# A reordered schedule line: the last two head groups of the first attention layer, row block 0 ahead of row block 1

## The chip, the cores and the metric

One NeuronCore of a Trainium2 chip runs the whole program. The metric is the device time in microseconds of one execution; several executions give a median. One more execution was recorded with the hardware profiler, and the trace rows below come from that one.

## The reference, cut to what matters

A decoder trunk of two layers works on 256 tokens of 1024 features, in float32. Layer 0 has causal attention with 16 heads of 64 (with 256 tokens there is one block, so the block-sparse attention is plain causal attention); layer 1 has differential attention. An MLP with 4096 hidden features follows each. Every sub-layer is modulated and closed in the same way:

```
mod = silu(c) @ ada_w + ada_b                       # six vectors of 1024 for each layer
for i in range(2):
    shift1, scale1, gate1, shift2, scale2, gate2 = split(mod[i], 6)
    h = x * (1 + scale1) + shift1
    y = attention(h) @ w_out                        # q, k, v = h @ w_in, rotary on 16 of 64 features
    x = layer_norm(alpha * x + (1 + gate1) * y)     # the closing of the attention
    h = x * (1 + scale2) + shift2
    y = square(relu(h @ w_up)) @ w_down
    x = layer_norm(alpha * x + (1 + gate2) * y)
```

## The kernel before, in words

The 256 tokens are two row blocks of 128, called b = 0 and b = 1. Each float32 product is made of three matmuls in a rounded format: every operand is split into a rounded part hi (ScalarE, L130 for weights) and a remainder lo (VectorE, L131), and hi·hi, hi·lo, lo·hi are accumulated. Weights come in by DMAs on SyncE's queue into three `raw` buffers; the split parts lie in eight `hi` and eight `lo` buffers of 128x1024.

`PROGRAM` is the order of the work, written out by hand, one string for each layer. A token is a step and its indices. `S0` to `S7` and `P`, `F` with the same numbers go through the pairs (b, g) in the order (0,0), (1,0), (0,1), (1,1), (0,2), (1,2), (0,3), (1,3), where g is a group of four heads; so even numbers are row block 0 and odd ones block 1.

- `Qbg`: the q and k columns of a group, 24 matmuls of 512 columns, then the rotary part on VectorE. `Tbg`: four transposes of the result.
- `Sn`: scores of the four heads (L417) into two banks with the tag `sc`, mask and maximum on VectorE (L381), exponential on ScalarE (L384).
- `Pn`: probabilities transposed (L397), copied by ScalarE (L399), multiplied with the values (L457), scaled on VectorE (L468). `Fn`: two transposes (L476), split into hi and lo (L482, L483).
- `Obh`: block b's part of the output product from head groups 2h and 2h+1, 24 matmuls (L184). `O00` and `O01` add up in two banks tagged `ac`, `O10` and `O11` in two tagged `sc`.
- `fN`: N steps of the filler. The filler is a list of the adaLN vectors: each step loads a 128x1024 piece of `ada_w` (L215, two buffers `aw`) and multiplies and sums it on VectorE (L216). For layer 0's attention the list holds GATE1, SCALE2, SHIFT2, eight pieces each. `B0` asks for what it needs of them (`need`), spreads the gate over the partitions (L115, L117), makes the columns A and B (L245 to L247) and loads `ln_g` and `ln_b`.
- `Cb0`: the closing of block b: gate and residual (L289, L292), statistics (L302, L303), the inverse root on GpSimd (L277, L278), normalisation (L308, L311), then eight transposes (L320), A and B applied by ScalarE (L324), and the split (L327, L328) into the tiles `hT` that the MLP multiplies.
- `Ubj`, `Xbj`, `Dbj`: the MLP's up product, its transposes and its down product for block b and columns j; `U` starts with L167.

The order of the string is not the order on an engine. It gives each instruction its rank; when the program is built, a planner walks through modelled time and gives each engine, among the instructions that it takes for ready, the one of the highest rank. From then on each engine works through its own list strictly in order. A buffer of a tag is handed out when its former user is done.

Of the kernel before, what the change touches and what calls it, by code (L numbers as in the profile page):

```python
# [44 lines left out]
PROGRAM = (  # L45
    """
    L0 V00 V10 Q00 T00 Q10 T10 Q01 T01 Q11 T11 S0 V01 f2 S1 f1 P0 S2 V11 f5 P1 F0 S3 P2 Q02 T02 f4 S4
    Q12 T12 f2 F1 f2 P3 S5 F2 Q03 T03 f4 P4 F3 S6 Q13 T13 f4 P5 F4 O00 P6 S7 F5 B0 P7 F6 F7 O01 C00 O10
    O11 C10 U00 U01 X00 U10 U11 X01 f1 X10 D00 f1 X11 Y2 f4 D10 f1 D01 f1 D11 Y3 f3 D02 f1 D12 Y4 f3 D03 f1
    D13 Y5 f3 D04 f1 D14 Y6 f3 D05 f1 D15 Y7 f2 D06 D07 B1 C01 D16 D17 C11  # L50
    """,
# [735 lines left out]
```

## Time and profile before

| what | value |
|---|---|
| three timed runs, us | 642.17, 645.62, 645.78 |
| median, us | 645.62 |
| the profiled execution, us | 644.11 |
| its span from first to last instruction, us | 640.7 |
| busy in the span: TensorE matmul, VectorE, ScalarE | 95%, 78%, 59% |

The span is what the trace shows; 3.4 us of the profiled execution's time lie outside it. PE is TensorE's matmuls, PEld its weight loads, which overlap them; DVE is VectorE, ACT ScalarE, POOL GpSimd and SPq SyncE's DMA queue. The matmuls are pipelined, so a row's duration (0.39 us for 512 columns) is longer than the distance to the next start.

### The profile page before, as it was taken

How to read it: one execution, taken by the hardware profiler on the slowest of the kernel's cores; microseconds unless marked ns; L12 is line 12 of the kernel's file. 1: busy time of each engine (PE TensorE's matmuls, PEld its weight loads, DVE VectorE, ACT ScalarE, POOL GpSimd, SP SyncE). 2: the span in 40 equal slices, each digit the busy share in tenths (PEclk: the TensorE clock that was granted, in tenths of full speed). 3: DMA queues.
4: the chain of work that ended last, by engine and by line, in shares of the span. 5: the costliest groups of instructions: out<-in, count | busy, mean ns of one | idle time of the engine just before them, and what ended most of it. 6: DMA issues, size and time to landing. Idle time of an engine off the chain costs nothing.

```text
span 640.7 us, 8768 instructions
## 1 busy us (share of the span) xinstructions
PE 609.0 (95%) x3140; PEld 499.6 (78%) x3140; DVE 500.4 (78%) x903; ACT 377.6 (59%) x699; POOL 22.2 (3%) x37
## 2 busy tenths in 40 slices
PE   4889999998999999999999999989999999999994
PEld 3667887886888888888877787767788888888883
DVE  5798998889978878888799989977984646465446
ACT  3448665657846545664477676765775556475530
POOL 0000000001000000000000010021100000000002
PEclk9999999999999999999999999999999999999998
DMA  8997998876689888989765967682663764746401
GB/s 292 406 322 279 313 325 286 288 250 227 215 309 343 308 313 330 326 294 338 268 231 188 337 229 263 232 289 68 208 218 109 259 225 143 255 133 213 182 0 66
DMA packets 65941, 158.23 MB, mean 247 GB/s; under 512 B 4041, under 2 KB 21098, under 8 KB 65898
## 3 DMA queue, kind: packets, MB, share of 16 engines
q1 hardware_dynamic: 65898, 157.68, 70.1%
q8 instruction: 24, 0.39, 0.2%
q14 instruction: 19, 0.16, 0.1%
HBM read 156.62 MB, written 1.05 MB: 246 GB/s over the span
## 4 chain that ended last, share of the span: by engine, by line
PE 64%; DVE 18%; DMA 6%; ACT 4%; issue 3%; POOL 2%; SPq 1%; DVEq 0%; POOLq 0%; ACTq 0%
PE ac L184 13%; PE sc L184 10%; PE mm L687 7%; PE tp L687 6%; DMA aw<-in_ada_w_dram 6%; DVE lo L131 5%; DVE aw L216 4%; PE mm L167 4%; PE mm L169 4%; PE mm L168 4%; PE mm L692 3%; PE tp L692 3%; ACT hi L130 2%; DVE z L292 1%; DVE z L289 1%
## 5 line engine op out<-in xcount | busy, mean ns | idle before, releaser
L131 DVE TENSOR_TENSOR lo<-raw,hi 128x1024 fp32r<-128x1024 f32 x196 | 232.0, 1197 | 44.1 <-ACT hi L130 40.4
L130 ACT CAST hi<-raw 128x1024 fp32r<-128x1024 f32 x196 | 201.3, 1034 | 62.5 <-PE sc L184 43.6
L216 DVE CUSTOM_DVE_ANT_0 aw<-aw,sbc,tabT 128x1024 f32<-128x1024 f32 x96 | 122.0, 1280 | 23.1 <-DMA aw<-in_ada_w_dram 22.7
L167 PE MATMUL mm<-hi,hT 128*128 128x512 f32 x224 | 90.6, 405 | 6.1 <-ACT hi L130 3.2
L169 PE MATMUL mm<-hi,hT 128*128 128x512 f32 x224 | 89.0, 398 | 0.0
L168 PE MATMUL mm<-lo,hT 128*128 128x512 f32 x224 | 88.6, 396 | 0.2 <-DVE lo L131 0.2
L687 PE MATMUL mm<-hT,hi 128*128 128x512 f32 x192 | 60.4, 396 | 0.0
L687 PE MATMUL tp<-hT,hi 128*128 128x512 f32 x192 | 60.3, 395 | 0.0
L167 PEld LDWEIGHTS mm<-hi,hT 128*128 128x128 f32 x224 | 42.3, 189 | 16.1 <-ACT hi L130 3.8
L184 PE MATMUL ac<-hi,sTh 128*128 128x512 f32 x160 | 51.2, 397 | 0.0
L184 PE MATMUL ac<-lo,sTh 128*128 128x512 f32 x160 | 50.8, 394 | 0.0
L184 PE MATMUL ac<-hi,sTl 128*128 128x512 f32 x160 | 50.4, 392 | 0.0
L169 PEld LDWEIGHTS mm<-hi,hT 128*128 128x128 f32 x224 | 42.3, 189 | 9.1 <-DVE hT L328 0.4
L168 PEld LDWEIGHTS mm<-lo,hT 128*128 128x128 f32 x224 | 42.3, 189 | 8.6 <-DVE lo L131 0.3
L184 PE MATMUL sc<-hi,sTh 128*128 128x512 f32 x144 | 45.3, 392 | 0.0
L184 PE MATMUL sc<-lo,sTh 128*128 128x512 f32 x144 | 45.1, 391 | 0.0
L184 PE MATMUL sc<-hi,sTl 128*128 128x512 f32 x144 | 44.6, 390 | 0.0
L692 PEld LDWEIGHTS tp<-hT,lo 128*128 128x128 f32 x192 | 34.4, 188 | 7.5
L692 PEld LDWEIGHTS mm<-hT,lo 128*128 128x128 f32 x192 | 34.4, 188 | 7.3
L697 ACT COPY nat<-mm 128x256 f32<-128x256 f32 x24 | 7.8, 376 | 52.4 <-PE mm L687 52.4
L692 PE MATMUL tp<-hT,lo 128*128 128x256 f32 x192 | 36.0, 279 | 0.0
L692 PE MATMUL mm<-hT,lo 128*128 128x256 f32 x192 | 35.9, 279 | 0.0
(153 smaller groups left out, 899.4 us busy)
## 6 DMA issues: line engine op xcount, KB each, us to landing
aw<-in_ada_w_dram SPq DMA_DIRECT2D x96, 512.0 KB, 5.5
raw<-in_mlp_w_up_dram SPq DMA_DIRECT2D x32, 1024.0 KB, 5.9
raw<-in_mlp_w_down_dram SPq DMA_DIRECT2D x32, 1024.0 KB, 5.1
raw<-in_diff_w_in_dram SPq DMA_DIRECT2D x16, 512.0 KB, 5.1
raw<-in_moba_w_in_dram SPq DMA_DIRECT2D x24, 256.0 KB, 5.5
raw<-in_moba_w_in_dram SPq DMA_DIRECT2D x8, 512.0 KB, 4.8
raw<-in_moba_w_out_dram SPq DMA_DIRECT2D x4, 1024.0 KB, 8.4
raw<-in_diff_w_in_dram SPq DMA_DIRECT2D x4, 1024.0 KB, 5.7
```

The costliest lines, as they stand in the source:

```text
L130: act.copy(out=hi[:, :n], in_=raw_ap)
L131: vec.tensor_tensor(out=lo[:, :n], in0=raw_ap, in1=hi[:, :n], op=ALU.subtract)
L167: pe.matmul(dst, lhsT=xh, rhs=wh, start=start, stop=False)
L168: pe.matmul(dst, lhsT=xh, rhs=wl, start=False, stop=False)
L169: pe.matmul(dst, lhsT=xl, rhs=wh, start=False, stop=stop)
L184: pe.matmul(dsts[h], lhsT=a, rhs=w[:, h * 512:(h + 1) * 512], start=start and k == 0 and i == 0, stop=stop and k == n - 1 and i == 2)
L216: vec.tensor_tensor_reduce(out=aw, in0=aw, in1=sbc, scale=1.0, scalar=adab_cols(l, v)[:, j:j + 1], op0=ALU.mult, op1=ALU.add, accum_out=dst)
L289: vec.tensor_tensor(out=z[:, c_], in0=accs[c_.start // 512][:, a0:a0 + c_.stop - c_.start], in1=gate[:, c_], op=ALU.mult)
L292: vec.scalar_tensor_tensor(out=z[:, c_], in0=xt[b][:, c_], scalar=ALPHA, in1=z[:, c_], op0=ALU.mult, op1=ALU.add)
L687: pe.matmul(ps, lhsT=w[k][0][:, c_], rhs=x3[k], start=first, stop=last)
L692: pe.matmul(ps[:, 0:S], lhsT=w[k][1][:, c_], rhs=x3[k][:, 0:S], start=False, stop=False)
L697: act.copy(out=r[:, i * S:(i + 1) * S], in_=ps[:, S:2 * S])
```

## The change

Only the third and fourth line of layer 0's string differ. The steps are the same and none is added or dropped; `F3`, `P5`, `F5`, `S7` and `Q13`, `T13` (block 1) go behind steps of block 0, and `C00`, which stood after all P and F, now stands ahead of `S7`.

```
     L0 V00 V10 Q00 T00 Q10 T10 Q01 T01 Q11 T11 S0 V01 f2 S1 f1 P0 S2 V11 f5 P1 F0 S3 P2 Q02 T02 f4 S4
-    Q12 T12 f2 F1 f2 P3 S5 F2 Q03 T03 f4 P4 F3 S6 Q13 T13 f4 P5 F4 O00 P6 S7 F5 B0 P7 F6 F7 O01 C00 O10
+    Q12 T12 f2 F1 f2 P3 S5 F2 Q03 T03 f4 P4 S6 F4 f4 O00 P6 Q13 F6 B0 O01 T13 F3 P5 C00 S7 F5 O10 P7 F7
     O11 C10 U00 U01 X00 U10 U11 X01 f1 X10 D00 f1 X11 Y2 f4 D10 f1 D01 f1 D11 Y3 f3 D02 f1 D12 Y4 f3 D03 f1
```

## Rows read from the trace of the kernel before

**Rows 1.** The page: busy time, share of the span, instructions.
```profile
PE 609.0 (95%) x3140; PEld 499.6 (78%) x3140; DVE 500.4 (78%) x903; ACT 377.6 (59%) x699; POOL 22.2 (3%) x37
```
**Rows 2.** Waits of PE, 50 to 640 us: us in total, times, longest.
```profile
PE tp L320 <- DVE nm L310: 1.8, 3, 1.0
PE tp L320 <- DVE z L308: 1.5, 3, 0.5
...
PE ac L457 <- ACT pT L399: 1.0, 1, 1.0
...
PE mm L168 <- DVE lo L131: 0.2, 1, 0.2
```
**Rows 3.** Timeline of PE at the closing: start, us, engine, line, operation.
```profile
143.24 0.62 PE L184 MATMUL sc<-hi,sTl 128*128 128x512 f32 x2
143.70 0.61 PE L184 MATMUL sc<-hi,sTh 128*128 128x512 f32 x2
145.27 0.63 PE L320 MATMUL tp<-cs,z 128*128 128x128 f32 x4 [0.96 <-DVE nm L310]
...
146.57 0.70 PE L184 MATMUL sc<-hi,sTl 128*128 128x512 f32 x2
148.40 0.50 PE L167 MATMUL mm<-hi,hT 128*128 128x512 f32 x1 [1.13 <-ACT hT L327]
```
**Rows 4.** Timeline of DVE at the closing.
```profile
123.00 0.42 DVE L381 CUSTOM_DVE_ANT_0 sc<-sc,cs 128x256 f32<-128x256 f32 x1
...
134.83 0.69 DVE L289 TENSOR_TENSOR z<-ac,gate 128x512 f32<-128x512 f32 x1 [0.52 <-PE ac L184]
...
141.32 1.28 DVE L216 CUSTOM_DVE_ANT_0 aw<-aw,sbc,tabT 128x1024 f32<-128x1024 f32 x1
...
143.73 0.16 DVE L247 TENSOR_TENSOR B<-B,col 128x8 f32<-128x8 f32 x1
144.58 0.55 DVE L308 TENSOR_SCALAR z<-z,bna,rs 128x512 f32<-128x512 f32 x1 [0.69 <-POOL rs L278]
```
**Rows 5.** Timeline of ACT: the last exponential of S7, and the closing.
```profile
126.18 0.46 ACT L384 ACTIVATE p<-sc,mx 128x256 f32<-128x256 f32 x1
...
146.01 1.83 ACT L324 ACTIVATE full<-tp,B,A 128x128 f32<-128x128 f32 x5
147.72 0.62 ACT L327 CAST hT<-full 128x512 fp32r<-128x512 f32 x1
```
**Rows 6.** Stages: PE, PEld, DVE, ACT, POOL busy; granted clock, DMA share, GB/s.
```profile
97.00:149.00 52.00, 48.13 (x299) 39.16 (x296) 43.90 (x100) 30.38 (x69) 1.65 (x2) 1.00 0.80 275
...
135.00:140.00 5.00, 5.00 (x24) 4.14 (x23) 4.54 (x8) 3.35 (x4) 0.00 (x0) 1.00 0.90 335
```
**Rows 7.** Timeline of PE: O00's first matmul and its ninth, Q13, S7, P7, F6.
```profile
101.01 0.47 PE L184 MATMUL ac<-hi,sTh 128*128 128x512 f32 x1
...
106.29 0.40 PE L184 MATMUL ac<-lo,sTh 128*128 128x512 f32 x1
...
108.06 0.48 PE L167 MATMUL mm<-hi,hT 128*128 128x512 f32 x1
...
113.97 0.39 PE L169 MATMUL mm<-hi,hT 128*128 128x512 f32 x1
...
121.53 1.16 PE L417 MATMUL sc<-qkT 64*128 64x128 f32 x16
...
129.40 1.89 PE L457 MATMUL mm<-v,pT 128*128 128x64 f32 x16
131.13 0.39 PE L476 MATMUL tp<-cs,on 128*128 128x128 f32 x2
```
**Rows 8.** The tile aw, 95 to 145 us: its operations, its landing.
```profile
L216 DVE CUSTOM_DVE_ANT_0 aw<-aw,sbc,tabT x13: 1274/1279/1286, 97.4 to 141.3; 128x1024 f32<-128x1024 f32 x13
...
DMA to landing us min/median/max: 4.0/4.9/5.5
```
**Rows 9.** Timeline of PE: the longest wait at the same place in layer 1.
```profile
432.91 0.44 PE L397 MATMUL tp<-cs,p 128*128 128x128 f32 x2 [0.85 <-DVE sTl L486]
```

## The prediction

> **What bounds the kernel now.** I read the page first [rows 1]: PE has matmuls in flight for 95% of the span, no other engine comes near. A high share alone does not say that PE is the limit, so the second view is the list of PE's waits after the first products [rows 2]: 14 rows from 1.8 down to 0.2 us, 10.5 us together. The reader is to see two things there: from 50 us on PE waits for almost nothing, so a reordering can give back some 10 us in all and not more; and the largest rows name the closing (z and nm). The third view is PE's timeline at layer 0's closing [rows 3]. Two matmuls of 512 columns take 0.46 us there (143.24 to 143.70), 0.23 each. O01's sums are done when the closing's first product starts, 134.83 [rows 4]; the first matmul of U00 starts at 148.40. Between them lie the dense matmuls of O10 and O11, and twice PE stands: 143.70 to 145.27 is 1.57 us for two matmuls worth 0.46, so 1.11 lost; 146.57 to 148.40 is 1.83 for 0.46, so 1.37 lost. The closing of block 0 (from O01's end to U00, 13.5 us) is a little longer than the work that covers it. This is what the change aims at, and it is 2.5 us.
>
> The fourth view, the stages [rows 6], is the warning: from 97 to 149 us DVE is busy 43.9 of 52 us, 84%. A closing is itself mostly DVE work. It does not move into a stretch where its engine rests.
>
> The Trainium skill (Perfetto Trace Analysis, Identifying the Most-Contended Engine) says that matmul busy time is a poor measure of how near TensorE is to its limit and that the busy share of the weight loads is a good one. By it the stretch has 25% of room, since PEld is busy 39.16 of 52 us; the fourth rival below prices that reading from rows.
>
> **The change part by part.** No instruction is added or removed, so every engine's sum stays; only positions move, and with them waits. The DMAs keep their order on SP's queue: the filler pieces of both f4, then the rows of w_out for O00, then the last two pieces and the two broadcast loads of B0, then the rows for O01, stand in that sequence in both strings. GpSimd has only the two short operations of each closing.
>
> (a) C00 ahead of S7, F5, P7, F7. What now covers it: O10 and O11 as before, 13.5 minus 2.5 us lost is 11.0 us of PE work, and in addition the pieces of block 1 that come after O01. S7 is 1.2 us, P7's 16 value matmuls are 1.73 us (129.40 to 131.13) [rows 7] and its 8 transposes about 0.9 by 0.11 each, so 2.6; P5 is the same shape, 2.6; two F some 0.2 each. That is 6.8 us, so the cover is 17.8 us. The chain is 13.5 us; if S7's mask and maximum on DVE (four operations of 0.42 us and a little more [rows 4]) all go in between, it is 15.4. Both are under 17.8: the two stalls go, minus 2.5 us.
>
> (b) What is late next: the column B. The shift needs the last of the 24 filler pieces. In the trace that product starts at 141.32 and B is made at 143.73 [rows 4], 0.85 us before the normalisation itself. ACT then needs four applications (0.37 each, 1.83 for five) and a cast of 0.62 [rows 5], 2.1 us, so U00 could start at 143.9 + 2.1 = 146.0. PE without its two stalls would be there at 148.4 - 2.5 = 145.9. So the saving of (a) just fits, if this stream stays where it is. It has two buffers: a landing of 4.9 us and a product of 1.28 give one piece each 3.1 us, while the 12 distances from 97.4 to 141.3 are 3.66 each [rows 8]. It could end 6.8 us earlier at best; if DVE takes the pieces later, it ends later. Were the transposes placed before B is there, ACT would stand at its first L324, and in its list behind that wait are the pT copies for P7 and the hi parts of the MLP's first weights, for which PE and DVE wait in turn. The second f4 has moved ahead of O00 and Q13 in rank, which speaks for a little earlier. I take no change, ends -0 and +2.5 (the whole of (a)).
>
> (c) Q13 behind O00 and P6. O00 was the filler that PE used from 101 to 127 us. At 108.06, when Q13 starts, 9 of its 24 matmuls are done (101.01 to 106.29) [rows 7] and 15 are left, 3.4 us; with P6's 1.3 us they now go first, so Q13 moves back by up to 4.7 us, from its end at 114.2 to 118.9, and T13 and S7 with it: S7 from 121.53 to at most 126.2. Its softmax ends 5.1 us after its scores start (121.53 to 126.64) [rows 5, 7], at most 131.3. Until then O10 cannot start, because its banks are those of the scores. What PE has between 118.9 and then: O01 5.5, P5 2.6, the gate's 8 transposes 0.9, T13 0.5, S7 1.2, F3 and F5 0.4, together 11.1 us, to 130.0. So between 0 and 1.3 us of new wait, and more where DVE lets the closing go ahead of S7's softmax: C00 has the higher rank now, and its two gate products, two additions, two statistics and one aggregate are at least 4.1 us (six of 0.69 by the first). Ends 0 and +5.4. The nearest row for a tail of this kind is the longest wait at the same place in layer 1, 0.85 us [rows 9], where the closing and the last P lie equally near each other. The planner sees the DVE conflict too and can put the softmax first when z is not ready. I take +0.5, near the lower end, for that reason.
>
> (d) The split of w_out's second half. Its hi buffers come free as Q13 uses up the group's weights, so these splits move back with Q13, and O01 with them; that is inside the 11.1 us of (c) and hides behind P5 and P6. At nothing if so; if not, it is the same starvation as in (c). More or fewer switches between kinds of matmul cost about 0.1 us each (0.48 us for the first matmul of Q13, 0.39 for its last [rows 7]); ten more or fewer is 1 us either way, taken as 0.
>
> (e) C10 keeps its cover: U00 and U01, 11.0 us behind O11, as before. The MLP and layer 1 keep their order. 0.
>
> Sum: -2.5 + 0 + 0.5 + 0 + 0 = -2.0 us. The profiled execution took 644.11 us with a span of 640.7, so the sum gives a span of 638.7 and 642.1 us. That execution lies 1.5 us under the median of the runs shown, 645.62; against the median the forecast is 643.6.
>
> The Trainium skill (Perfetto Trace Analysis, Optimization Strategy) says that interleaving regimes with different most-contended engines can improve performance. Here the row speaks half against it: after PE, DVE is the busiest engine on both sides of the interleaving [rows 6], so by the rule the gain would be the full 2.5 us, by the row 2.5 less what DVE gives back.
>
> **The rivals.** First, **the shift stream holds the closing** (b): z is ready early, but B is not, or the planner's ready times give nearly the old order on the engines. Then PE waits at U00 as it does now and the time is 645.6, within 1 us. For it: B lies 0.85 us ahead of the normalisation today. Against it: the arithmetic of (b) leaves room for 2.4 us.
>
> Second, on the other side, **PE starves between O01 and O10**: S7's softmax stands behind C00 on DVE, the banks stay taken, and O00, which used to fill such holes, is spent. Price: 1.3 + 4.1 us of new wait. It decides from the point where S7's last exponential ends later than 130.0 us, when PE has used up O01 and P5. With the 2.5 saved it is +2.9, 648.5; if the stream of (b) also slips and nothing is saved, +5.4, 651.0. For it: DVE at 84% and the lost filler. Against it: the planner ranks only what is ready, so the softmax goes first wherever z is not.
>
> Third, **all waits of the region go**: besides the 2.5 us also the wait of 0.96 for pT and the smaller ones [rows 2], and a microsecond of switches. That is up to -5, 640.6.
>
> Fourth, **PE is far from full**: the weight loads fill only 75% of the stretch, so a better mixture could pack it tighter by 12.8 us, 632.8. Against it: in 135 to 140 us PE waits for nothing, starts a matmul each 0.23 us or less, and PEld is busy 4.14 of 5 us [rows 6], so 83% is full here and the room is 52 - 39.16 / 0.83 = 4.8 us. This is the reading of the page named above, and by it the trace disagrees as far as 100% is taken for full.
>
> **How the numbers follow.** The forecast (-1 to -4) has 0.50, the stream rival 0.22, starvation 0.20, all waits gone 0.06, the fourth 0.02. The likeliest gives 643.6. Runs of the same kernel spread by 3.6 us (642.17 to 645.78). The lower end of the range is 640.6 less a microsecond of that spread, 639.5; the upper takes in the first price of starvation, 648.5, and a microsecond, 649.5. Outside are about 1 in 10 above and 1 in 10 below. Faster by over 1% means below 639.2, slower means over 652.1; 1% is about what a measurement of this kernel can tell from no change. Faster: the fourth rival and the edge of the third, 0.06. Slower: both of starvation's parts together and more, 0.07. Within: 0.87.
>
> **What would show it.** Right: in PE's timeline no wait for nm at the first L320 and none for hT at the first L167 of the MLP, which starts at about 146 us; L289 on `ac` before S7's L381 or among them; P7 and F7 later than the start of C00. B's L247 still at 141 to 144. Wrong by (b): L320 early, then L324 on ACT waiting for B. Wrong by (c): a wait of PE of over 1 us between 118 and 132, ended by an exponential, a pT copy or a lo, and fewer than 15 matmuls of O00 left to fill. The forecast fails altogether if the waits after 165 us change, which no part of this argument expects.

## The result, and the profile after

The changed kernel takes 652.16 us (median of four runs, 651.08 to 653.29); the kernel before, in runs beside it, 644.77 (642.17 to 645.78). The ratio on record is 1.0137, 95% interval 1.0105 to 1.0169 (the two medians alone give 1.0115): slower by over 1%, and outside the predicted range. The profiled execution took 653.29 us with a span of 651.2, 10.5 longer than before.

The page, busy line and the line of the granted clock (one digit for each fortieth of the span):

```profile
PE 612.3 (94%) x3140; PEld 502.0 (77%) x3140; DVE 501.3 (77%) x903; ACT 377.4 (58%) x699; POOL 20.9 (3%) x37
PEclk9999999969999999999999999999999999999998
```

Against [rows 1] the instructions are the same and the engines' sums nearly so; PE has 3.3 us more, and one slice, around 140 us, has a 6 where before all but the last have 9. The waits of PE, 50 to 651 us:

```profile
PE tp L320 <- DVE z L308: 8.5, 4, 7.2
PE tp L320 <- DVE nm L310: 2.4, 2, 1.8
PE tp L397 <- ACT full L324: 1.5, 1, 1.5
PE ac L457 <- ACT pT L399: 1.0, 1, 1.0
```

In [rows 2] no wait for z was longer than 0.5 us; now one is 7.2, and there is a new kind, P7's transposes (L397) for a bank that ScalarE still reads (releaser `full`, L324). PE's timeline, to be held against [rows 3] and [rows 7]:

```profile
127.62 1.16 PE L417 MATMUL sc<-qkT 64*128 64x128 f32 x16
128.71 1.10 PE L457 MATMUL mm<-v,pT 128*128 128x64 f32 x8
129.65 0.61 PE L397 MATMUL tp<-cs,p 128*128 128x128 f32 x4
130.99 1.10 PE L457 MATMUL mm<-v,pT 128*128 128x64 f32 x8 [0.73 <-ACT pT L399]
139.29 2.09 PE L320 MATMUL tp<-cs,z 128*128 128x128 f32 x8 [7.20 <-DVE z L308]
141.17 1.46 PE L184 MATMUL sc<-hi,sTh 128*128 128x512 f32 x2
...
148.19 0.43 PE L476 MATMUL tp<-cs,on 128*128 128x128 f32 x2
150.08 0.66 PE L397 MATMUL tp<-cs,p 128*128 128x128 f32 x4 [1.47 <-ACT full L324]
...
155.54 0.40 PE L167 MATMUL mm<-hi,hT 128*128 128x512 f32 x1
```

Read it downwards. S7's scores come at 127.62 (121.53 before). After P5's last values, at 132.1, PE starts nothing until 139.29, when the closing's eight transposes go; O10 begins at 141.17; P7's transposes, which stood before the closing (127.71), come at 150.08, and U00 at 155.54 instead of 148.40. Not everything lacked its input in that hole: F5's is ready on VectorE at 132.8 (L468 below), but its two transposes come behind the closing's and the 24 matmuls of O10, at 148.19. VectorE shows why S7 was not done:

```profile
125.91 0.69 DVE L289 TENSOR_TENSOR z<-ac,gate 128x512 f32<-128x512 f32 x1 [1.12 <-PE ac L184]
...
130.60 1.28 DVE L292 SCALAR_TENSOR_TENSOR z<-x,z 128x512 f32<-128x512 f32 x2
...
132.40 0.40 DVE L468 TENSOR_TENSOR on<-mm,sums 128x256 f32<-128x256 f32 x1
...
133.32 1.27 DVE L216 CUSTOM_DVE_ANT_0 aw<-aw,sbc,tabT 128x1024 f32<-128x1024 f32 x1
...
136.28 1.28 DVE L216 CUSTOM_DVE_ANT_0 aw<-aw,sbc,tabT 128x1024 f32<-128x1024 f32 x1 [1.68 <-DMA aw<-in_ada_w_dram]
...
137.61 0.41 DVE L381 CUSTOM_DVE_ANT_0 sc<-sc,cs 128x256 f32<-128x256 f32 x1
...
144.97 0.16 DVE L247 TENSOR_TENSOR B<-B,col 128x8 f32<-128x8 f32 x1
```

The scores are complete at about 128.8, but the first mask and maximum (L381) runs at 137.61: the additions and statistics of C00 stand ahead of it, and between them filler products, the last of which waits 1.68 us for its own DMA while everything behind it waits too. Until the exponentials are done the two `sc` banks stay S7's and O10 has nowhere to go. ScalarE's part:

```profile
138.11 0.47 ACT L384 ACTIVATE p<-sc,mx 128x256 f32<-128x256 f32 x1 [7.17 <-DVE mx L381]
...
144.28 1.05 ACT L130 CAST hi<-raw 128x1024 fp32r<-128x1024 f32 x1 [2.49 <-PE sc L184]
145.67 1.06 ACT L130 CAST hi<-raw 128x1024 fp32r<-128x1024 f32 x1 [0.33 <-PE sc L184]
146.62 1.85 ACT L324 ACTIVATE full<-tp,B,A 128x128 f32<-128x128 f32 x5
```

The transposes are done at 141.4, but L324 needs B, which is made at 144.97, after the last filler product; and on ScalarE two casts of weights (L130) go ahead of it, so that it starts at 146.62. Until ScalarE has read the transposes (the first bank at about 148.1, four of the five of L324; the second at 150.0), both `tp` banks are taken, and F5 and P7 wait for them: P7's last exponential ends at 141.7 (141.22 and 0.47), its transposes run at 150.08. Last, the windows (PE, PEld, DVE, ACT, POOL busy, granted clock, DMA share, GB/s):

```profile
130.00:135.00 5.00, 1.36 (x11) 0.99 (x9) 4.60 (x9) 0.58 (x1) 0.00 (x0) 0.88 0.75 275
135.00:140.00 5.00, 0.71 (x4) 0.71 (x4) 3.10 (x11) 1.17 (x3) 0.79 (x2) 0.50 0.89 311
140.00:145.00 5.00, 5.00 (x16) 3.57 (x16) 4.16 (x10) 2.40 (x8) 0.00 (x0) 0.60 0.14 44
```

Behind the hole the clock is at 0.50 (1.2 GHz), and O10's first matmuls run at that level: in 140 to 145 us PE has 16 matmuls, small transposes among them, in [rows 6] 24 in as long a window.

**The account.** For each kernel I take the start of Y2's first matmul (L687 here), up to which the same PE work is done in all, and add up PE's waits from 101 us to it; for the clock, PE's busy time in each window of 1 us times one minus the granted clock. The column of the clock is an estimate from those rows.

```
kernel                     Y2's first   waits   lost to clock   span
before                       179.34      3.9        0           640.7
after                        189.57     11.4        2.4         651.2
s7_before_c00                189.55      8.8        4.7         650.3
q13_early                    190.12     10.3        4.0         651.2
softmax_first                189.91      6.8        6.0         652.3
transposes_late              186.21      7.9        1.6         647.8
transposes_after_f7          185.64      8.3        1.9         646.7
softmax_and_transposes       182.11      3.1        3.3         643.0
c00_after_f7                 183.02      3.3        3.3         643.9
no_shift_in_b                191.61     11.8        3.9         652.4
q13_early_both               180.28      2.5        0           645.2
closing_parts_only           176.46      1.2        0           637.2
closing_between_o01_p7       176.96      1.7        0           639.6
c00_alone_early              188.74      9.7        3.4         649.5
```

From before to after Y2 comes 10.2 us later: 7.5 of waits, 2.4 of clock, 0.3 of the rest. The spans differ by 10.5, so nearly the whole loss lies ahead of Y2, in this region.

### The profile page after: what moved, and what is told of

Same layout as the page of the kernel before. It is cut to its first block, busy times and chain, and to the rows that moved or that the text cites. A ratio compares the mean times of both kernels' runs of the same rounds, so it can differ in the third digit from the quotient of the medians.

```text
span 651.2 us, 8767 instructions
## 1 busy us (share of the span) xinstructions
PE 612.3 (94%) x3140; PEld 502.0 (77%) x3140; DVE 501.3 (77%) x903; ACT 377.4 (58%) x699; POOL 20.9 (3%) x37
## 5 line engine op out<-in xcount | busy, mean ns | idle before, releaser
L130 ACT CAST hi<-raw 128x1024 fp32r<-128x1024 f32 x196 | 200.9, 1035 | 61.7 <-PE sc L184 43.6
L687 PE MATMUL mm<-hT,hi 128*128 128x512 f32 x192 | 60.4, 396 | 0.0
L687 PE MATMUL tp<-hT,hi 128*128 128x512 f32 x192 | 60.3, 395 | 0.0
L384 ACT ACTIVATE p<-sc,mx 128x128 f32<-128x128 f32 (+1 forms) x64 | 26.6, 420 | 20.3 <-DVE mx L381 17.9
```

The costliest lines, as they stand in the source:

```text
L130: act.copy(out=hi[:, :n], in_=raw_ap)
L384: act.activation(out=pt[:, :n], in_=sc, func=AF.Exp, bias=mx, scale=-1.0, accum_out=sums[:, scol_i:scol_i + 1])
L687: pe.matmul(ps, lhsT=w[k][0][:, c_], rhs=x3[k], start=first, stop=last)
```

## The experiments

All strings are cut from layer 0's; the change alters one line of it, the second, and the experiments edit the same stretch. Up to q13_early_both each diff is against the changed kernel. Each ratio is to the kernel before in the runs of the same session, whose median was 643.98 us for the first four runs put on record (s7_before_c00, q13_early, softmax_first, transposes_late), 643.13 for the next four and 643.84 for the last four (q13_early_both and the three from the kernel before); so times of different sessions are best compared by these ratios. The theories grew with the runs. A is that S7's softmax is late and holds the `sc` banks. D, formed after the first four runs, is that the closing's transposes hold PE's list and the `tp` banks ahead of P7; E is the clock. B and C are told in the expectations that name them.

**s7_before_c00**: S7 ranked ahead of the closing.

```
-    O01 T13 F3 P5 C00 S7 F5 O10 P7 F7
+    O01 T13 F3 P5 S7 C00 F5 O10 P7 F7
```

> The changed kernel with one swap: S7 is ranked ahead of the closing C00. Theory A (S7's mask and maximum stand on VectorE behind the closing and four filler products, so its score banks stay taken and O10 cannot start): the softmax now stands between the filler products, its last exponential comes about 4 us sooner, PE's wait of 7.2 us shrinks to 2 to 4 us, time 645 to 648. Theory B (PE's list has the eight transposes of the closing ahead of O10): they now stand behind most of O10, time 645 to 648 too. Theory C (Q13 comes later, so S7's scores do, and O00 is used up): S7's scores stay at 127 to 128 us and PE runs dry as before, time 650 to 653.

653.64 us, ratio to before 1.0137 (1.0093 to 1.0181). Miss. L381 runs at 130.42 to 136.09, and the 7.2 us wait for z is gone, but PE waits 3.4 for the softmax, 2.5 and 1.2 for L324, and P7's transposes come at 148.33. A alone is not it.

**q13_early**: S7's input early as well, C00 still ahead of S7.

```
-    P4 S6 F4 f4 O00 P6 Q13 F6 B0 O01 T13 F3 P5 C00 S7 F5 O10 P7 F7
+    P4 S6 Q13 T13 F4 f4 O00 P6 F6 B0 O01 F3 P5 C00 S7 F5 O10 P7 F7
```

> The changed kernel with Q13 and T13 back ahead of F4, O00 and P6; the closing is still ranked ahead of S7. Theory A: S7's scores come at about 121 us, before the closing has anything to do on VectorE, so its softmax does not wait although C00 outranks it; 643 to 646. Theory C: the same, 643 to 646. If the rank of C00 alone were the cause, 650 to 653.

654.82 us, 1.0154 (1.0098 to 1.0211). Miss; the nearest of the cases named is the last, the rank of C00. L381 is at 123.07 to 127.99, little later than before (123.00 to 125.54), and yet (PE):

```profile
141.24 2.09 PE L320 MATMUL tp<-cs,z 128*128 128x128 f32 x8 [4.25 <-DVE z L308]
...
146.46 0.69 PE L476 MATMUL tp<-cs,on 128*128 128x128 f32 x2 [3.13 <-ACT full L324]
148.38 1.11 PE L397 MATMUL tp<-cs,p 128*128 128x128 f32 x4 [1.23 <-ACT full L324]
```

and on ScalarE:

```profile
144.90 1.86 ACT L324 ACTIVATE full<-tp,B,A 128x128 f32<-128x128 f32 x5 [2.74 <-DVE B L247]
```

P7's probabilities have been there since about 129. PE stands 4.25 us at the closing's transposes, which are next in its list, then for the banks, which wait for B. Theory D comes from this run.

**softmax_first**: the changed kernel's string, S7's mask, maximum and exponential ranked ahead of all.

```
-            ps_ = [softmax(b, sc[i, cpt], sums, 2 * i + cpt) for i in range(2) for cpt in range(2)]
+            with tc.high_priority() if (b, g) == (1, 3) else nullcontext():
+                ps_ = [softmax(b, sc[i, cpt], sums, 2 * i + cpt) for i in range(2) for cpt in range(2)]
```

> The changed kernel with the mask, maximum and exponential of S7 at high priority and the string as changed. Theory A: the four L381 follow the scores directly, O10 starts at about 132 us, no wait of PE above 2 us, 643 to 646. Theory C: S7's scores still come at 127 to 128 us, PE has used up O01 and P5 at 132, so a wait of about 1 to 2 us stays, 645 to 648. The granted clock stays at its upper level in both.

653.46 us, 1.0127 (1.0081 to 1.0173). Miss. The waits fall to 6.8 us, but P7's transposes still come at 147.73, ended by L324, and more is lost to the clock than anywhere else, 6.0.

**transposes_late**: C00 in two; the vector part stays in place, and the transposes with all behind them become a step `M`, which calls `rest`.

```
         z = layer_norm(
...
-        modulate(b, z, A, B, tiles)
-        filler.appendleft(lambda: residual(b, z, gb, bb))
+        def rest():
+            modulate(b, z, A, B, tiles)
+            filler.appendleft(lambda: residual(b, z, gb, bb))
...
-    P5 C00 S7 F5 O10 P7 F7
+    P5 C00 S7 F5 O10 M P7 F7
```

> The changed kernel with C00 in two: its VectorE part where it was, its transposes and what follows ranked behind O10. Theory A: nothing changes, since O10 still waits for the score banks; 651 to 653, and PE waits 7 us. Theory B: O10 outranks the transposes, the wait goes, 643 to 646. Theory C: as A.

651.61 us, 1.0110 (1.0057 to 1.0164): the time that theory A gives. Theory B, as it is put here, fell: O10 still could not start, because its banks were S7's, so seven of the transposes went ahead of it at 137.61 after 5.07 us of wait, and P7 came at 145.75.

**transposes_after_f7**: the same, with M behind P7 and F7.

```
-    P5 C00 S7 F5 O10 P7 F7 O11
+    P5 C00 S7 F5 O10 P7 F7 M O11
```

> The changed kernel with C00 in two: the VectorE part where it was, the transposes and what follows ranked behind F7. Theory D (the closing's eight transposes take both transposing banks and hold them until ScalarE can apply the column B, which the last filler product makes at 143 to 145 us; P7's transposes queue behind them, so P7, F7, half of O11 and C10 come 10 us and more later): P7's transposes come at 138 to 142 us and not at 150, the second half of the loss goes, 646 to 649. The wait of 5 to 7 us for the score banks stays (theory A). If A alone counted, 651 to 653.

649.98 us, 1.0089 (1.0055 to 1.0123): a part of the loss goes, less than expected (646 to 649). P7's transposes start at 136.50, 13.6 us earlier than in the changed kernel; what PE now waits for is the softmax, 3.94 and 1.30 us.

**softmax_and_transposes**: s7_before_c00 and transposes_after_f7 together.

```
-    P5 C00 S7 F5 O10 P7 F7 O11
+    P5 S7 C00 F5 O10 P7 F7 M O11
```

> As transposes_after_f7, and S7 ranked ahead of the closing's VectorE part as well. A and D together: neither the wait for the score banks (over 2 us) nor that for the transposing banks is left, P7 starts by 137 us, the granted clock stays at its upper level or falls for less than 4 us, 642 to 647. If a third cause keeps the kernel slow (Q13 later and O00 used up), 649 or more.

646.45 us, 1.0040 (1.0021 to 1.0059). Held in time, waits and P7, but not for the clock, which falls for longer than the 4 us allowed. Softmax alone leaves 8.8 us of waits, transposes alone 8.3, both 3.1, less than the kernel before. Against s7_before_c00 (1.0137) this run moves the closing's transposes and nothing else, and Y2 comes 7.4 us sooner: the cleanest single test of their place. And it is still 2.8 us late at Y2. The windows show the rest:

```profile
129.00:130.00 1.00, 0.30 (x3) 0.06 (x1) 1.00 (x5) 0.61 (x2) 0.00 (x0) 1.00 0.80 291
130.00:131.00 1.00, 0.97 (x8) 0.97 (x8) 0.90 (x2) 0.90 (x4) 0.00 (x0) 1.00 1.05 217
131.00:132.00 1.00, 0.48 (x5) 0.35 (x4) 0.44 (x2) 0.00 (x0) 0.00 (x0) 1.00 0.84 268
132.00:133.00 1.00, 0.53 (x5) 0.29 (x3) 1.00 (x1) 0.75 (x2) 0.00 (x0) 0.96 0.92 344
133.00:134.00 1.00, 0.74 (x4) 0.74 (x4) 1.00 (x5) 0.49 (x2) 0.00 (x0) 0.50 0.98 377
```

and PE, in the stretch at 0.50 and behind it:

```profile
135.56 0.63 PE L184 MATMUL sc<-lo,sTh 128*128 128x512 f32 x1
135.99 0.63 PE L184 MATMUL sc<-hi,sTl 128*128 128x512 f32 x1
...
140.03 0.40 PE L184 MATMUL sc<-lo,sTh 128*128 128x512 f32 x1
140.26 0.39 PE L184 MATMUL sc<-hi,sTl 128*128 128x512 f32 x1
```

O00 and O01 are used up by 125 us, and P5, S7 and the first half of P7 follow each other as transposes and products of 64 columns, with short gaps between them. At 133 the clock is at 0.50, and O10's matmuls start every 0.43 us instead of every 0.23, until 139.6.

**c00_after_f7**: the closing back behind all P and F, and O10 with it; the rest of the change kept.

```
-    P5 C00 S7 F5 O10 P7 F7 O11
+    P5 S7 F5 P7 F7 C00 O10 O11
```

> The changed string with C00 put behind F7, so that the closing is asked for after the last scores and values as in the kernel before, while Q13, F3, P5 and O01 keep their new places. A and D: P7 is no longer behind the closing on either engine, P7 by 136 us, 642 to 647. If the late Q13 and the spent O00 are the cause, 649 to 653.

646.48 us, 1.0024 (1.0000 to 1.0049). Held; the interval just reaches no change, though Y2 is 3.7 us late. Without the early closing 8.1 of the 11.4 us of waits are gone, and 3.3 are left; the clock is at 0.50 from about 134 to 141 here too, so that loss needs no early closing.

**no_shift_in_b**: the changed kernel, but layer 0's MLP input lacks its shift.

```
-        vec.tensor_tensor(out=B, in0=B, in1=cols[sh], op=ALU.add)
+        if (l, first) != (0, False):
+            vec.tensor_tensor(out=B, in0=B, in1=cols[sh], op=ALU.add)
```

> The changed kernel, its string as it is, with the shift left out of the column B of the first MLP's input: the filler products are still made, but B no longer waits for them. This leaves out the addition of SHIFT2 for all of layer 0's MLP input. Theory D: ScalarE applies A and B as soon as the transposes are done, at about 140 us, the banks come free 5 us sooner, P7 at 142 to 144 us; 647 to 650. Theory A: the wait for z and the score banks is as before, 650 to 653.

654.12 us, 1.0160 (1.0125 to 1.0196). Miss. Lines are one higher here; PE:

```profile
138.34 2.09 PE L321 MATMUL tp<-cs,z 128*128 128x128 f32 x8 [6.53 <-DVE z L309]
141.16 0.69 PE L477 MATMUL tp<-cs,on 128*128 128x128 f32 x2 [0.73 <-ACT full L325]
143.07 1.11 PE L398 MATMUL tp<-cs,p 128*128 128x128 f32 x4 [1.22 <-ACT full L325]
...
152.23 0.61 PE L398 MATMUL tp<-cs,p 128*128 128x128 f32 x4
```

The banks come free 7 us earlier than with B, and P7's first half moves to 143.07, as expected. But the 6.53 us for z remain, P7's second half stays at 152, behind O10's matmuls in PE's list, and the clock costs 3.9 us. So the wait for B sets how long the banks are held, and is not what the time hangs on. That the place of the transposes is, transposes_after_f7 and softmax_and_transposes show.

**q13_early_both**: softmax_and_transposes with Q13 early, so that dense products lie between the small ones again.

```
-    P4 S6 F4 f4 O00 P6 Q13 F6 B0 O01 T13 F3 P5 S7 C00 F5 O10 P7 F7 M
+    P4 S6 Q13 T13 F4 f4 O00 P6 F6 B0 O01 F3 P5 S7 C00 F5 O10 P7 F7 M
```

> As softmax_and_transposes, and Q13 and T13 back ahead of F4, O00 and P6, so that P5, S7 and P7 have dense matmuls of O00, O01 and O10 between them again. Theory E (what is left of the loss in softmax_and_transposes and c00_after_f7 is TensorE's clock: P5, S7 and P7 stand together there, ten us of transposes and 64-column matmuls with short gaps, and the granted clock falls to 0.5 for 6.8 us, 3.3 us of busy time): the clock stays at its upper level, PE's waits stay at 3 to 4 us, 640 to 644. If the clock falls here too, 645 to 648.

644.46 us, 1.0014 (0.9990 to 1.0039): just above the 640 to 644 expected, and not told from the kernel before. The clock stays at 1.00 through the region. At Y2 it stands 0.9 us behind before, with waits 1.3 lower; the 2.3 us between have no single row. The profiled execution was the longest of its twelve (647.25), and loses more at a later closing, C01. On VectorE, where C01's L289 is queued behind this product:

```profile
320.14 1.28 DVE L216 CUSTOM_DVE_ANT_0 aw<-aw,sbc,tabT 128x1024 f32<-128x1024 f32 x1 [5.61 <-DMA aw<-in_ada_w_dram]
```

PE waits 3.1 us for nm there (330.03), and the clock is at 0.76 and 0.81 in the two windows of 4 us from 328. The wait for that piece was 3.75 us before. Whether other executions lose there too is open.

The last three start from the kernel before and keep Q13, T13, P5 and F4 where they were. Each diff is against before.

**c00_alone_early**: C00 whole ahead of S7, with F6, B0 and O01 before it and O10 ahead of P7.

```
-    O00 P6 S7 F5 B0 P7 F6 F7 O01 C00 O10 O11
+    O00 P6 F6 B0 O01 C00 S7 F5 O10 P7 F7 O11
```

> The order of the kernel before for Q13, T13, P5 and O00, with F6, B0, O01 and the whole closing C00 ahead of S7, F5 and P7: one part of the change alone. Theory D: the closing's transposes again hold both transposing banks until B is there, P7 starts near 148 us, PE waits and the clock falls; 648 to 653. If the late Q13 and the spent O00 were needed for the loss, 642 to 646.

651.98 us, 1.0134 (1.0101 to 1.0167). Held: this part of the change alone gives the whole loss.

```profile
141.83 1.11 PE L320 MATMUL tp<-cs,z 128*128 128x128 f32 x4 [4.34 <-DVE z L308]
...
147.83 1.11 PE L397 MATMUL tp<-cs,p 128*128 128x128 f32 x4 [1.23 <-ACT full L324]
```

S7 is early here and O10 starts at 131.99, yet PE stands 4.34 us at L320 with P7 behind it, whose last exponential ended at 131.8, and P7 then waits for the banks.

**closing_parts_only**: the closing's vector part behind S7, its transposes behind F7.

```
-    O00 P6 S7 F5 B0 P7 F6 F7 O01 C00 O10 O11
+    O00 P6 F6 B0 O01 S7 C00 F5 O10 P7 F7 M O11
```

> The order of the kernel before as far as Q13, T13, P5 and O00 go; only F6, B0, O01 and the closing's VectorE part move ahead of S7's values, S7 ranked before that part, and the transposes stay behind F7. Theory E: dense matmuls between the pieces of block 1, the clock stays up; 640 to 644. The prediction's own 2.5 us (no wait for nm or hT at the closing) should show here, so 641 to 642 if all of it comes through.

640.86 us, 0.9971 (0.9943 to 0.9999). Held: it beats the changed kernel (1.0137) by about 1.6%, and the kernel before by a margin whose interval only just ends below 1.

```profile
135.43 0.60 PE L397 MATMUL tp<-cs,p 128*128 128x128 f32 x4
...
141.94 0.60 PE L320 MATMUL tp<-cs,z 128*128 128x128 f32 x4
...
143.79 0.60 PE L320 MATMUL tp<-cs,z 128*128 128x128 f32 x4
...
146.08 0.39 PE L167 MATMUL mm<-hi,hT 128*128 128x512 f32 x1
```

L320 and U00 have no wait before them, where [rows 3] has 0.96 and 1.13. P7 goes 6.5 us ahead of the transposes, and U00 starts at 146.08 instead of 148.40.

**closing_between_o01_p7**: S7 where it was, the vector part between O01 and P7.

```
-    O00 P6 S7 F5 B0 P7 F6 F7 O01 C00 O10 O11
+    O00 P6 S7 F5 B0 F6 O01 C00 P7 F7 M O10 O11
```

> The kernel before with F6 and O01 ahead of P7, the closing's VectorE part behind O01, its transposes behind F7; the rest as before. The smallest move of the closing. The clock stays up; 641 to 644; if the column B sets the start of the MLP, no faster than before, 643 to 645.

642.50 us, 0.9981 (0.9956 to 1.0005). Held in size, not told from no change. U00 starts at 145.70.

## Why the prediction was wrong

**What bounds the kernel** held: the loss is PE's holes and its clock, and nothing else carries it (7.5 and 2.4 of 10.2 us).

**(a) is the step that failed: its cover of 17.8 us.** The size of the saving was about right: in closing_parts_only, where P7 and O10 really cover the closing, U00 comes at 146.08, 2.3 us earlier, where (b) had 146.0 at best, and the span is 3.5 shorter. But the step set work against chain as if PE could take whatever is ready. It can't: in the changed kernel the eight L320 come ahead of O10, F5 and P7, and O10 lacks its banks besides. From the closing's first product (125.91) to the first L320 (139.29) PE is busy for 5.0 of 13.4 us, and 7.2 of the rest are the wait for z; in the kernel before the same stretch (134.83 to 145.27) has 9.5 busy of 10.4, in closing_parts_only (129.96 to 141.94) 11.7 of 12.0. So some 5 us stood ahead of the waiting instruction, and not 17.8.

**(b) failed with it.** It said what would happen if the transposes were placed before B is there, and put it at ScalarE's list; then it took 0, because B hardly moves. B did hardly move (143.73 to 144.97). The closing's transposes moved to 139.29, and what the step did not ask is what they hold while they wait: both `tp` banks, which P7 needs (1.47 us of PE's wait here, 4.36 with F5 in q13_early). no_shift_in_b shows that B is only part of it. What the place of the transposes costs is shown by s7_before_c00 against softmax_and_transposes (1.0137 and 1.0040, 7.4 us at Y2), transposes_after_f7 against the changed kernel (1.0089 and 1.0137, 3.9 us at Y2), and c00_alone_early against closing_parts_only, 11.1 us, where S7 goes ahead of the closing too. Each of these moves both the place in PE's list and the turn at the `tp` banks, so the runs do not tell the two apart.

**(c) was mis-sized.** Q13 ended at 118.9, as written, and the scores came at 127.62, 1.4 us past the bound. The softmax was to end at 131.3 and ended at 141.7. The step counted 4.1 us of the closing on VectorE; it left out the filler products between them (133.32, 136.28 and most of one before, 1.28 each) and the 1.68 us in which VectorE itself stood for a DMA. Taken +0.5, upper end +5.4; measured, a wait of 7.2, in which the late z and the late softmax lie on top of each other. The step also read one row wrongly: O00 was done by 121.3 us in the kernel before, and what PE had up to 127.9 was the first half of O01. The argument that the planner puts the softmax first wherever z is not ready did not hold: L381 ran after all of C00's additions and statistics.

**(d)** shows no wait of its own, and the switches stayed small (0.3 us of rest in the account). **(e)** held in its cost: C10's first L320 comes at 168.09, 12.1 us later than before, because F7 and O11 are late with P7, but its own wait is 0.25 us, where it was 0.47.

**The clock** was in no step. [rows 6] show 1.00, and I took that for given; it costs 2.4 us in the changed kernel, by the estimate above.

**The rivals.** The second, starvation between O01 and O10, named the right place and sign, with 651.0 at its upper price. Its remedy is not the whole: with the softmax early in three different ways the time stays at 653 to 655. Of the first rival the condition came, B made 5.7 us after the first half of z (144.97 and 139.24), but not its time of 645.6. The third did not come; of the fourth nothing is seen.

**The signs.** The one for (b), L320 early and L324 held until B, came (139.29 and 146.62). The wait of (c) came at 132.1 to 139.3, just behind the stretch named, and ended by z. Behind Y2 PE's waits are 5.2 us before and 5.9 after, so the loss does lie where the argument looked.

The Trainium skill (Perfetto Trace Analysis, Optimization Strategy) says that interleaving regimes may improve performance. The runs show both outcomes: the interleaving of this string costs 1.37%, and closing_parts_only, with the bank-holding part behind P7, is at 0.9971.

## What to carry to other kernels

When a step is moved forward on an engine with an in-order list, ask not only whether its chain is covered but what it holds while it waits: its place in the list and the buffers that it has taken. Move forward the part that needs time (here the vector part) and leave the part that takes shared banks behind the work that wants them. And count as cover only what stands ahead of the waiting instruction.

## What the runs showed of the hardware

The granted clock fell to 0.50 (1.2 GHz) without a long wait. In softmax_and_transposes no wait from 101 us to Y2 is over 0.73 us and all together are 3.1, and yet PE ran at 0.50 from 133 to 139.6 after four windows with busy 0.30, 0.97, 0.48 and 0.53. The kernel before has busy 0.31, 0.73, 1.00, 0.27 and 0.60 from 144 to 149 us and stays at 1.00, so how much it takes is open. The Trainium skill (TensorE: Matmul & The Clock Gate, Part 1) says that a gate halves the array's clock according to how busy it has been, and gives 426.7 and 215.7 ns between matmuls of 512 columns at the two levels; the trace has 0.43 and 0.23 us, so it agrees at the lower level and is 0.01 us longer at the upper.
